# Last six rows as one-row chains, and no VectorE products in the last 16 rows, in a sum of reciprocals

## The chip, the core and the metric

One core of one Trainium2 chip. The metric is the device time of one execution in microseconds (us), smallest is best. Row numbers are those of one partition: each of the 128 partitions holds 128 rows of 1024 numbers, and "row 126" means row 126 of all partitions at once (0.5 MB).

## The reference

```python
def setup_inputs():
    batch, seq, dim = 32, 512, 1024
    return {"x": np.abs(np.random.randn(batch, seq, dim)).astype(np.float32) + 1e-6}

def reference(x):
    return np.sum(1.0 / x, axis=-1).astype(np.float32)
```

67.1 MB come in, 64 KB go out.

## The kernel before

A row's 1024 numbers are split into two halves of 512, a and b, and 1/a + 1/b is computed as (a + b) / (ab), so that ScalarE does its Ln and Exp on 512 products instead of 1024 numbers. Four engines share the rest:

- the product ab: GpSimd, or for some rows VectorE. For a product on VectorE, PE first puts b into PSUM (the memory that PE writes its results to) with two passes of an identity matrix (tile `b`);
- Ln and Exp(-.): ScalarE, giving 1/(ab), in PSUM (`r`) or in place (`pr`);
- the sum: either PE first adds a + b (four passes, tile `s`, in PSUM too) and VectorE multiplies and sums 512 numbers (0.68 us), or VectorE multiplies and sums all 1024 itself (1.22 us).

A chunk is a triple (m, e, v): m rows, of which e are added by PE, and v have their product on VectorE. Loads are lists of chunks; A, B and C are pairs of rows. All loads go into a ring of 40 rows.

```python
    SINGLE = 124
    A, B, C = (2, 0, 0), (2, 2, 0), (2, 2, 1)
    LOADS = [[A, B, A, B], [A, B, A, C]] * 5 + [[A, B, A, C]]
    LOADS += [[A, B], [A, C]] * 3 + [[A], [B], [A], [C]] * 2
    # (cut)
    for chunks in LOADS:
        n = sum(m for m, _, _ in chunks)
        xt = ring[:, c0 % R : c0 % R + n, :]
        keep(nc.sync.dma_start(out=xt, in_=x_v[:, c0 : c0 + n, :]))
        made, q = [], 0
        for m, e, v in chunks:
            pr = ppool.tile([P, m, H], f32, tag="ps" if e else "pr")
            for j in range(v):                      # products on VectorE
                b = bpool.tile([P, H], f32, tag="b")
                add(b, xt[:, q + j, H:])            # PE
                i = nc.vector.tensor_tensor(out=pr[:, j, :], in0=xt[:, q + j, :H], in1=b, op=mult)
            # (cut)
        for (m, e, v), pr in zip(chunks, made):
            # (cut) product of the other rows on GpSimd, then for e rows:
            #       add(s, xc[:, j, :H], xc[:, j, H:])   on PE
            if waiting:
                sum_rows(*waiting)                  # VectorE, chunk before
            keep(nc.scalar.activation(out=pr, in_=pr, func=Ln, scale=S))
            step = 1 if c0 + q >= SINGLE else m
            # (cut) Exp of the m - e other rows into PSUM, of the e rows in place
            waiting = c0 + q, xc, pr, sm, rc
```

Rows 0 to 111 come in loads of eight and four rows, rows 112 to 127 in eight loads of two. Each engine runs its own instructions in the order in which this loop makes them.

## Time and profile before

| | kernel before |
|---|---|
| time, median of 3 runs | 171.8 us (171.78 to 171.88) |
| span of the profiled run | 169.98 us |
| last load landed | 161.04 us |
| last sum on VectorE done | 167.10 us |
| output's store and closing after it | 2.88 us |

The first line of the page gives each engine's busy time and its share of the span:

```profile
PE 131.9 (78%) x278; PEld 50.8 (30%) x278; DVE 122.5 (72%) x267; ACT 134.1 (79%) x131; POOL 138.3 (81%) x70
```

No engine is full, because the loads are (93% of the span). In such a kernel a late change can only move what lies between the last landing and the end. I call that distance, from the last landing to the end of VectorE's last accumulator read, **the tail**: 6.06 us here.

### The profile page before, as it was taken

The page shows a single profiled execution, that of the slowest core. Times are in us where ns is not written, and L with a number is a line of the kernel's source. Part 1 is how long each engine was busy: PE and PEld are TensorE (multiplying, and loading weights), DVE is VectorE, ACT ScalarE, POOL GpSimd, SP SyncE. Part 2 cuts the span into 40 slices and gives each one's busy share as a digit, 9 for nine tenths or more (in the row PEclk, how much of TensorE's full clock was granted, in tenths as well). Part 3 has the DMA queues.
Part 4 walks back from the last instruction along what each step waited for, and adds up shares of the span by engine and source line. Part 5 has one row for each costly group of instructions (what it writes and reads, how often), then busy time and mean ns, then how long its engine had stood idle before and what let it go on. Part 6 is the DMA issues. An engine that isn't in the chain of part 4 may idle for free.

```text
span 170.0 us, 1264 instructions
## 1 busy us (share of the span) xinstructions
PE 131.9 (78%) x278; PEld 50.8 (30%) x278; DVE 122.5 (72%) x267; ACT 134.1 (79%) x131; POOL 138.3 (81%) x70
## 2 busy tenths in 40 slices
PE   0008899786988789784999869798879999998790
PEld 0003333231332233231443313233333334333230
DVE  0000777767987677767687679878789898989883
ACT  3002989978887988958889787888999999999890
POOL 1008999699996999689996998979999999998920
PEclk9999999999999999999599999999999999999999
DMA  6999999999999999999999999999999999999400
GB/s 208 409 455 409 463 401 463 409 455 409 463 411 455 409 455 405 447 418 440 424 440 424 440 424 441 397 420 422 428 432 432 428 416 418 414 422 428 175 0 15
DMA packets 3750, 67.24 MB, mean 396 GB/s; under 512 B 416, under 2 KB 544, under 8 KB 544
## 3 DMA queue, kind: packets, MB, share of 16 engines
q1 hardware_dynamic: 3744, 67.18, 92.9%
q8 instruction: 2, 0.03, 0.1%
q14 instruction: 4, 0.03, 0.0%
HBM read 67.11 MB, written 0.07 MB: 395 GB/s over the span
## 4 chain that ended last, share of the span: by engine, by line
DMA 63%; POOL 15%; ACT 10%; issue 4%; DVE 3%; PE 3%; DVEq 0%; POOLq 0%; SPq 0%
DMA ring<-in_x_dram 63%; POOL pr L143 15%; ACT pr L154 6%; PE s L84 2%; DVE ring L94 2%; ACT r L162 2%; ACT pr L169 2%; DVE pr L94 1%; PE b L84 1%; DVE pr L132 0%; DVEq L202 0%; DVE sums L94 0%; POOLq L143 0%; SPq L124 0%; DVEq L94 0%
## 5 line engine op out<-in xcount | busy, mean ns | idle before, releaser
L143 POOL TENSOR_TENSOR pr<-ring 128x1024 f32<-128x1024 f32 x64 | 137.6, 2185 | 23.5 <-DMA ring<-in_x_dram 23.2
L84 PE MATMUL s<-ring,ident 128*128 128x512 f32 x256 | 122.4, 616 | 32.2 <-DVE sums L94 16.2
L154 ACT ACTIVATE pr<-pr 128x1024 f32<-128x1024 f32 x64 | 67.3, 1052 | 28.6 <-POOL pr L143 28.5
L84 PEld LDWEIGHTS s<-ring,ident 128*128 128x128 f32 x256 | 46.8, 193 | 104.6 <-issue 62.1
L94 DVE CUSTOM_DVE_ANT_1 pr<-ring,r 128x1024 f32<-128x1024 f32 x31 | 37.9, 1221 | 43.3 <-ACT r L162 43.1
L94 DVE CUSTOM_DVE_ANT_0 pr<-pr,s 128x512 f32<-128x512 f32 x64 | 41.4, 684 | 0.6 <-PE s L84 0.5
L94 DVE CUSTOM_DVE_ANT_1 ring<-ring,r 128x1024 f32<-128x1024 f32 x33 | 40.1, 1217 | 0.0
L169 ACT ACTIVATE pr<-pr 128x1024 f32<-128x1024 f32 (+1 forms) x33 | 33.9, 1031 | 1.0
L162 ACT ACTIVATE r<-pr 128x1024 f32<-128x1024 f32 (+1 forms) x33 | 33.0, 1001 | 1.0
L84 PE MATMUL b<-ring,ident 128*128 128x512 f32 x22 | 12.3, 639 | 1.6 <-DMA ring<-in_x_dram 1.5
L94 DVE DVE_READ_ACCUMULATOR2_ANT sums<- 128x1 f32 x128 | 10.6, 83 | 0.0
L132 DVE TENSOR_TENSOR pr<-ring,b 128x512 f32<-128x512 f32 x11 | 7.5, 684 | 0.8 <-PE b L84 0.7
L84 PEld LDWEIGHTS b<-ring,ident 128*128 128x128 f32 x22 | 4.0, 201 | 9.4 <-DMA ring<-in_x_dram 7.5
L55 ACT ACT_TABLE_LOAD x1 | 1.3, 1283 | 0.7 <-PEq L191 0.7
masks.py:197 POOL MEMSET ident<- 128x128 f32 x1 | 0.2, 205 | 0.3 <-POOLq L191 0.3
masks.py:199 POOL TENSOR_SCALAR_AFFINE_SELECT ident<-ident 128x128 f32<-128x128 f32 x1 | 0.3, 294 | 0.1
L191 POOL MEMSET const-float32-0.0<- 128x1 f32 x1 | 0.1, 99 | 0.2 <-issue 0.2
L191 POOL MEMSET const-bfloat16-1.0<- 128x1 bf16 x1 | 0.1, 102 | 0.0
L191 POOL MEMSET const-uint8-127<- 128x1 uint8 x1 | 0.1, 102 | 0.0
L191 POOL MEMSET const-float32-1.0<- 128x1 f32 x1 | 0.1, 99 | 0.0
## 6 DMA issues: line engine op xcount, KB each, us to landing
ring<-in_x_dram SPq DMA_DIRECT2D x11, 4096.0 KB, 37.7
ring<-in_x_dram SPq DMA_DIRECT2D x6, 2048.0 KB, 36.8
ring<-in_x_dram SPq DMA_DIRECT2D x8, 1024.0 KB, 28.3
out_dram<-sums SPq DMA_DIRECT2D x1, 64.0 KB, 1.5
```

Source lines behind the costliest of these rows:

```text
L55: nc.scalar.add_instruction(mybir.InstLoadActFuncSet(name=nc.get_next_instruction_name(), act_func_set_id=act_sets.index("natural_log_exp_ ...
L84: i = nc.tensor.matmul(bank, lhsT=ident, rhs=half, start=k == 0, stop=k == len(halves) - 1,)
L94: i = nc.vector.tensor_tensor_reduce(out=row if out is None else out, in0=row, in1=fac, scale=S, scalar=0.0, op0=mult, op1=plus, accum_out ...
L132: i = nc.vector.tensor_tensor(out=pr[:, j, :], in0=xt[:, q + j, :H], in1=b, op=mult)
L143: i = nc.gpsimd.tensor_tensor(out=pr[:, v:, :], in0=xc[:, v:, :H], in1=xc[:, v:, H:], op=mult)
L154: keep(nc.scalar.activation(out=pr, in_=pr, func=Ln, scale=S))
L162: nc.scalar.activation(out=r, in_=pr[:, j:to, :], func=Exp, scale=-1.0)
L169: keep(nc.scalar.activation(out=r, in_=r, func=Exp, scale=-1.0))
L191: nc = _bacc.Bacc("TRN2", target_bir_lowering=False, num_devices=1)
```

## The change

The intent: the last rows pass through the engines one by one, so that the last row doesn't wait for its pair, and VectorE and PE are rid of the products in the last 16 rows (rows 118 and 126), which GpSimd takes instead.

```diff
-    SINGLE = 124
     A, B, C = (2, 0, 0), (2, 2, 0), (2, 2, 1)
+    L, S1 = (1, 0, 0), (1, 1, 0)
     LOADS = [[A, B, A, B], [A, B, A, C]] * 5 + [[A, B, A, C]]
-    LOADS += [[A, B], [A, C]] * 3 + [[A], [B], [A], [C]] * 2
+    LOADS += [[A, B], [A, C]] * 3 + [[A], [B], [A], [B], [A]]
+    LOADS += [[L, S1], [S1, S1], [L, S1]]
 (cut: the special case of SINGLE in sum_rows)
-            step = 1 if c0 + q >= SINGLE else m
             rc = []
-            for j in range(e, m, step):
 (cut: with one row to a chunk, one Exp of m - e rows and one of e rows do)
```

More of the change, by code (lines that the diff above doesn't have):

```diff
@@ L113, in sum_rows @@
                 rc[j - e].unsqueeze(1).to_broadcast([P, 2, H]),
-                pr[:, e : e + 2, :] if j == e and e + 1 < m and c < SINGLE else None,
+                pr[:, e : e + 2, :] if j == e and e + 1 < m else None,
             )
@@ L154 @@
             keep(nc.scalar.activation(out=pr, in_=pr, func=Ln, scale=S))
-            step = 1 if c0 + q >= SINGLE else m
             rc = []
-            for j in range(e, m, step):
-                to = min(j + step, m)
-                r = rpool.tile([P, to - j, H], f32, tag="rc")
+            if e < m:
+                r = rpool.tile([P, m - e, H], f32, tag="rc")
                 keep(
-                    nc.scalar.activation(
-                        out=r, in_=pr[:, j:to, :], func=Exp, scale=-1.0
-                    )
-                )
-                rc += [r[:, l, :] for l in range(to - j)]
-            for to in range(e, 0, -step):
-                r = pr[:, max(to - step, 0) : to, :]
+                    nc.scalar.activation(out=r, in_=pr[:, e:, :], func=Exp, scale=-1.0)
+                )
+                rc = [r[:, l, :] for l in range(m - e)]
+            if e:
+                r = pr[:, :e, :]
                 keep(nc.scalar.activation(out=r, in_=r, func=Exp, scale=-1.0))
```

## The prediction

> **What bounds the kernel now.** I read the page of the whole span first, then the chain that ended last, then the groups with shapes kept apart, then the last 30 us as a timeline by engine. The page, transfers by slice (40 slices of 4.25 us) and the load queue:
>
> ```profile
> DMA  6999999999999999999999999999999999999400
> q1 hardware_dynamic: 3744, 67.18, 92.9%
> ```
>
> The transfers never pause from the first slice until slice 37. The landing records of the last eight loads (two rows of each partition, 1 MB) stand at 143.67, 146.16, 148.65, 151.13, 153.62, 156.10, 158.58 and 161.04 us: one each 2.48 us, 1.24 us a row, 1.05 MB per 2.48 us = 423 GB/s. So the first 161.04 us are the memory's. The chain that ended last, in order of time, says what follows:
>
> ```profile
> 141.21 19.84 DMA ring<-in_x_dram
> 161.04 0.04 issue
> 161.09 1.12 PE b L84 x2
> 162.21 3.45 PE s L84 x8
> 165.66 0.03 issue
> ...
> 165.79 0.11 DVE pr L94
> ...
> 166.49 0.60 DVE pr L94
> 167.09 0.01 DVE sums L94
> ```
>
> The last load waits in the queue for 19.84 us, so nothing that compute does late in the kernel delays it. After it come PE's sum of one row's halves for VectorE's product (b), PE's sums of both last rows (s), then two sums on VectorE; the output leaves at 167.13, and 2.85 us of store and closing follow to 169.98. Only 167.10 - 161.04 = 6.06 us can be won here.
>
> Durations come from the groups by shape:
>
> ```profile
> L143 POOL TENSOR_TENSOR pr<-ring 128x1024 f32<-128x1024 f32 x53 | 124.2, 2372 | 23.4 <-DMA ring<-in_x_dram 23.2
> L94 DVE CUSTOM_DVE_ANT_0 pr<-pr,s 128x512 f32<-128x512 f32 x64 | 41.4, 684 | 0.6 <-PE s L84 0.5
> L169 ACT ACTIVATE pr<-pr 128x512 f32<-128x512 f32 x2 | 1.1, 622 | 0.0
> L162 ACT ACTIVATE r<-pr 128x512 f32<-128x512 f32 x2 | 1.1, 592 | 0.0
> L143 POOL TENSOR_TENSOR pr<-ring 128x512 f32<-128x512 f32 x11 | 14.1, 1283 | 0.1
> L132 DVE TENSOR_TENSOR pr<-ring,b 128x512 f32<-128x512 f32 x11 | 7.5, 684 | 0.8 <-PE b L84 0.7
> ```
>
> A product of two rows on GpSimd takes 2.37 us, of one row 1.28; in a row they start 2.33 and 1.24 apart (their records overlap by 0.04). The third view is GpSimd's timeline near the end:
>
> ```profile
> 141.26 11.86 POOL L143 TENSOR_TENSOR pr<-ring 128x1024 f32<-128x1024 f32 x6
> 153.75 8.72 POOL L143 TENSOR_TENSOR pr<-ring 128x1024 f32<-128x1024 f32 x4 [0.63 <-DMA ring<-in_x_dram]
> ```
>
> GpSimd ran behind the transfers until 153.12, then waited 0.63 us for rows 120 and 121. It catches up only because row 118's product was VectorE's: 2 rows cost it 1.24 us there, not 2.33. This slack is what the change spends.
>
> **What the Trainium skill says.** "ScalarE: Activation LUTs", section "What ACT_TABLE_LOAD costs", gives an activation with immediates as 186 ns + 0.833 ns per element, with about 93 ns of overlap back to back: 1039 ns for 1024 elements, 613 for 512. The trace agrees: 1028 to 1059 and 582 to 629. Halving the width thus doesn't halve the time. "GPSIMD Engine Reference", section "3.1 Elementwise — side-by-side cycle accounting", has about 2.6 cycles an element at two inputs, 2.17 ns at 1.2 GHz; the trace's (2372 - 1283) / 512 is 2.13 ns, which leaves 0.19 us for each instruction. "SBUF — State Buffer", section "SBUF: two separate sides", says that a VectorE instruction with two SBUF inputs shuts GpSimd out, and one with a PSUM input does not. Every two-input VectorE instruction here reads one input from PSUM, and all eleven short products of GpSimd took 1272 to 1295 ns, beside a busy VectorE: no blocking is seen. "DMA: Bandwidth & Descriptors", section "Measured (HBM→SBUF, 128 partitions, SWDGE, issued from GpSimd)", has 425 GB/s for a large transfer; 423 here from another issuing queue: the stream has no reserve.
>
> **The change part by part.** The order of instructions shows that rows 0 to 117 and the 25 loads (sizes and order) stay as they were; the two kernels differ from row 118 on.
>
> Removed: VectorE's products of rows 118 and 126 (2 x 0.68 us) and, on PE, their b sums (2 x 0.86 us: two passes per half at 0.43 us a start). The second one stands on the final chain. Of the last load, PE now sums row 127 alone: 4 passes, 1.72 us, instead of 12 passes. Rows summed on PE stay 64. So PE would be done near 163 if nothing else held it.
>
> Added to GpSimd: 2.33 - 1.24 = 1.09 us at rows 118/119; row 126's product, 1.24 us; and rows 122/123 and 124/125 as single products, (2 x 1.24 - 2.33) = 0.15 us each time. Together 2.63 us, of which its pauses after 153 (1.12 us by the single starts, 0.63 of them in the line above) take up a part. GpSimd, from the start of rows 118/119 at 151.85 in the trace: next starts 154.18 (rows 120/121), 156.51 (122), 157.75 (123), 158.99 (124), 160.23 (125), 161.47 (126), 162.71 (127), done 163.99 (162.48 + 2.63 - 1.12). Each of its rows has landed by then, so it never waits again; six single rows at 1.24 are exactly as fast as the transfers. In the kernel before its last product ended at 162.48.
>
> ScalarE: six more activations (131 to 137 instructions). A dependent pair starts Ln then Exp 0.66 us apart (0.63 and the 0.03 us hand-over seen from 163.27 + 1.04 to 164.34), and the next Ln 0.54 after that Exp (164.34 to 164.88 in the trace): 1.20 us a row against 2.05 for two rows. Rows 120/121: Ln at 156.58 after GpSimd, Exp 157.67. Row 122's Ln then waits for ScalarE, not GpSimd, and starts 157.67 + 0.97 = 158.64. From there 1.20 each: 123 at 159.84, 124 at 161.04, 125 at 162.24, 126 at 163.44, 127 at 164.64. Last Exp from 165.30 to 165.93.
>
> VectorE: rows 120/121 at 158.73 and 159.88, then row 122 at 161.02 (1.15 a start), 123 at 162.17, 124 at 162.78, 125 at 163.56 (its Exp), 126 at 164.73 (its Exp), 127 at 165.96, done with the read of the accumulator at about 166.65. That last start is set almost equally by ScalarE (165.96) and by VectorE's own row 126 (164.73 + 1.15 = 165.88). PE's sum of row 127 needs one of three buffers, the one row 123 frees at about 162.8: 162.85 + 1.72 + 0.17 = 164.7, before 165.9, so PE leaves the path.
>
> Sum: VectorE ends at 166.65 instead of 167.10, 0.45 us earlier. Off the path go about 4.6 us of PE; in their place stand GpSimd's lateness and ScalarE's six rows. 171.8 - 0.45 = 171.35.
>
> **The rivals.** First, that GpSimd is no queue at all and the tail is only landing, one product, Ln, Exp and sum: 161.04 + 2.52 + 1.3 + 0.7 = 165.5, a gain of 1.6 us (170.2). For it speaks the wait of 0.63 us at 153.12; against it that the change removes the cause of this wait. Second, that ScalarE's chain is slower than mine or that VectorE loses its overlap: the built order shows that the single-row sums on VectorE wait for PE, for ScalarE and for VectorE itself, one wait more than the two-row ones had. If each costs 0.1 us in VectorE's chain (the pause between wait and start at 165.69 to 165.79), or each Exp 0.1 us more, the gain is lost or turns into +0.3 us (172.1). Against it: these waits are for old work and are passed while ScalarE is waited for. Third, that PE's wait for row 123's buffer ends last; it has 1.2 us in hand, so VectorE would have to be that late. Fourth, that transfers stop earlier or later: the last load is issued at 141.21, before any changed row, so I give this nothing beyond 0.1 us of scatter (the three runs span 171.78 to 171.88).
>
> **Range and chances.** 171.4 us, half-way between my sum and the second rival's small costs. The range 170.7 to 172.0 takes in most of the first and second rival. For faster by over 2% the time must fall under 168.4, which needs 3.4 of the 6.06 us behind the last landing; two products of GpSimd, Ln, Exp and a sum alone are 4.5 us. Chance 0.01. Slower by over 2% needs 3.4 us more on some engine in the tail, 0.01. The rest, 0.98, is within 2%.
>
> **What would show each step.** Right: the last landing stays at 161.0 (within 0.1); GpSimd doesn't pause after 153 and ends at about 164.0; ScalarE runs without pause from about 158.6 to 165.9; VectorE's last sum ends at 166.4 to 166.9, and the final chain goes through ScalarE or GpSimd with no PE in it. Wrong: a landing that moved; a wait of GpSimd for a load after 154; PE's s among the last waits; single Ln or Exp far from 0.63 us; or a VectorE chain with gaps of over 0.1 us between sums whose Exp was ready.

## The result and the profile after

171.06 us (median of 6 runs, 170.92 to 171.21) against 171.84 (6 runs, 171.75 to 172.23): ratio 0.9951, 95% interval 0.9939 to 0.9964, within 2%. A ratio in this document is the mean time of one kernel's fast runs over that of the other's fast runs of the same rounds, so not quite the ratio of the medians. The gain is 0.8 us; the prediction's sum had been 0.45 us, its stated time 171.4.

The chain that ended last, from GpSimd's product of rows 120/121 on (start, duration, what):

```profile
154.12 2.40 POOL pr L144
156.52 0.02 issue
156.54 1.06 ACT pr L155
...
158.59 0.62 ACT pr L155
159.21 0.02 issue
159.24 0.60 ACT r L160
...
163.96 0.18 ACT r L160
...
164.69 0.20 DVE ring L95
...
165.92 0.60 DVE pr L95
166.52 0.01 DVE sums L95
```

PE is gone from it. GpSimd hands over to ScalarE at rows 120/121, and from 156.54 ScalarE does nothing but its own work to the end: Ln at 158.59 is row 122's, Exp at 163.96 row 126's. VectorE's two last sums follow. GpSimd's timeline shows that it no longer pauses for a load; one merged piece runs from 138.88 to 163.91:

```profile
138.88 25.03 POOL L144 TENSOR_TENSOR pr<-ring 128x1024 f32<-128x1024 f32 x14
```

PE's timeline for the last three rows that it adds; the second piece is row 127, which had to wait for a PSUM buffer (0.57 us by the bracket, until VectorE had read row 123's) and is still done at 164.85, before row 127's Exp:

```profile
158.62 3.67 PE L85 MATMUL s<-ring,ident 128*128 128x512 f32 x8 [0.53 <-DMA ring<-in_x_dram]
162.87 1.98 PE L85 MATMUL s<-ring,ident 128*128 128x512 f32 x4 [0.57 <-DVE sums L95]
```

The one-row instructions in the groups by shape (count, then busy us, mean ns, and idle us before them):

```profile
L144 POOL TENSOR_TENSOR pr<-ring 128x512 f32<-128x512 f32 x15 | 19.0, 1286 | 0.0
L155 ACT ACTIVATE pr<-pr 128x512 f32<-128x512 f32 x6 | 3.7, 613 | 0.0
L165 ACT ACTIVATE pr<-pr 128x512 f32<-128x512 f32 x4 | 2.5, 630 | 0.1
```

Every duration is the one that the prediction used, within 3%. The tail is 5.60 us (160.93 to 166.53), so the path from the last landing is worth 6.06 - 5.60 = 0.46 us, almost exactly the predicted 0.45. The remaining 0.3 to 0.4 us are not on that path. The span behind the last sum holds the store of the sums and a closing exchange between the engines; I call it **the closing**: 2.88 us before, 2.51 after. VectorE runs two drain instructions there: the first starts while its last sums run and ends 0.05 us behind them, the second is part of the exchange. In the listing of the closing's instructions, VectorE's drains read (least, middle, most ns of the two; first and last start in us):

```profile
L202 DVEq DRAIN  x2: 130/602/1074, 166.1 to 169.6; - x2
```

before, and after:

```profile
L198 DVEq DRAIN  x2: 19/392/764, 165.8 to 168.6; - x2
```

The last drain takes 19 ns instead of 130 and, counted from the last sum, starts 2.09 us instead of 2.53 us later. Nothing in the change is meant to do this. So the experiments had two questions: which part of the change is worth the 0.46 us, and where the closing's 0.37 us come from.

### The profile page after: what moved, and what is told of

It is laid out like the page before. It is cut to its first block, busy times and chain, and to the rows that moved or that the text cites. A ratio compares the mean times of both kernels' runs of the same rounds, so it can differ in the third digit from the quotient of the medians.

```text
span 169.0 us, 1265 instructions
## 1 busy us (share of the span) xinstructions
PE 130.5 (77%) x274; PEld 49.9 (30%) x274; DVE 121.1 (72%) x265; ACT 134.7 (80%) x135; POOL 140.7 (83%) x73
## 4 chain that ended last, share of the span: by engine, by line
DMA 52%; POOL 22%; ACT 13%; issue 8%; DVE 3%; POOLq 0%; DVEq 0%; SPq 0%
DMA ring<-in_x_dram 52%; POOL pr L144 22%; ACT pr L155 8%; ACT r L160 2%; ACT pr L165 2%; DVE ring L95 2%; DVE pr L95 1%; DVE pr L133 0%; DVE sums L95 0%; POOLq L144 0%; DVEq L198 0%; SPq L125 0%
## 5 line engine op out<-in xcount | busy, mean ns | idle before, releaser
L144 POOL TENSOR_TENSOR pr<-ring 128x1024 f32<-128x1024 f32 (+1 forms) x67 | 140.0, 2130 | 22.6 <-DMA ring<-in_x_dram 22.6
L155 ACT ACTIVATE pr<-pr 128x1024 f32<-128x1024 f32 (+1 forms) x67 | 67.9, 1013 | 28.2 <-POOL pr L144 28.2
L165 ACT ACTIVATE pr<-pr 128x1024 f32<-128x1024 f32 (+1 forms) x34 | 34.2, 1007 | 1.1
L85 PE MATMUL b<-ring,ident 128*128 128x512 f32 x18 | 10.0, 639 | 0.0
L133 DVE TENSOR_TENSOR pr<-ring,b 128x512 f32<-128x512 f32 x9 | 6.1, 683 | 0.7 <-PE b L85 0.7
L85 PEld LDWEIGHTS b<-ring,ident 128*128 128x128 f32 x18 | 3.4, 205 | 6.2 <-DMA ring<-in_x_dram 4.3
```

The costliest lines, as they stand in the source:

```text
L85: i = nc.tensor.matmul(bank, lhsT=ident, rhs=half, start=k == 0, stop=k == len(halves) - 1,)
L144: i = nc.gpsimd.tensor_tensor(out=pr[:, v:, :], in0=xc[:, v:, :H], in1=xc[:, v:, H:], op=mult)
L165: keep(nc.scalar.activation(out=r, in_=r, func=Exp, scale=-1.0))
```

## The experiments

Theory: the tail was PE's (two passes for b, eight for s, then two sums), the change replaces it by ScalarE's one-row chain, which starts late because GpSimd is late. Rivals: fewer VectorE products are worth something in themselves; PE's passes alone are the gain; GpSimd's last two products or the last landing still set the end; and for the rest of the time, scatter.

Twelve runs were made, eleven other kernels and the changed kernel again; all gave correct results, each timed in five rounds against nine runs of the kernel before on the same chip (three groups of four, on three chips). The edits of e1 and p1 are to the kernel before, that of p3 is to e2, all others are to the changed kernel; some are printed shortened. Tail and closing are from each kernel's one trace; records are the entries in VectorE's stream there, waits and drains included.

| run | median us (before) | ratio, 95% interval | tail us | VectorE records | closing us |
|---|---|---|---|---|---|
| kernel before | | | 6.06 | 321 | 2.88 |
| changed kernel | 171.06 (171.84) | 0.9951, 0.9939 to 0.9964 | 5.60 | 319 | 2.51 |
| e1, row 118 to GpSimd only | 171.71 (171.75) | 0.9992, 0.9979 to 1.0004 | 6.06 | 319 | 2.57 |
| e2, row 118 back on VectorE | 170.83 (171.75) | 0.9944, 0.9931 to 0.9956 | 5.23 | 321 | 2.81 |
| e3, single rows in the last load only | 171.87 (171.75) | 1.0006, 0.9993 to 1.0018 | 6.36 | 319 | 2.50 |
| e4, row 126 back on VectorE | 172.00 (171.75) | 1.0007, 0.9993 to 1.0020 | 6.28 | 321 | 2.81 |
| changed kernel again | 171.08 (171.83) | 0.9958, 0.9944 to 0.9971 | 5.55 | 319 | 2.51 |
| e5, pairs exchanged | 170.88 (171.83) | 0.9943, 0.9930 to 0.9955 | 5.38 | 319 | 2.50 |
| e6, e2 with loads of one row | 170.91 (171.83) | 0.9946, 0.9933 to 0.9958 | 5.21 | 321 | 2.87 |
| e7, rebalanced | 171.23 (171.83) | 0.9964, 0.9952 to 0.9977 | 5.87 | 323 | 2.51 |
| p1, before + 2 memsets | 171.46 (171.85) | 0.9978, 0.9965 to 0.9990 | 6.06 | 323 | 2.57 |
| p2, changed + 2 memsets | 171.28 (171.85) | 0.9968, 0.9955 to 0.9980 | 5.59 | 321 | 2.81 |
| p3, e2 + 2 memsets | 170.71 (171.85) | 0.9931, 0.9919 to 0.9944 | 5.25 | 323 | 2.51 |
| p4, spread | 170.72 (171.85) | 0.9932, 0.9918 to 0.9945 | 5.13 | 324 | 2.52 |

In each of these runs, the change of the tail plus the change of the closing gives the measured difference of mean times to within 0.2 us (least well in e3, -0.08 against +0.11 us, and e1, -0.31 against -0.13). So one trace's tail and closing say where the time goes, but not to the hundredth.

### e1: row 118's product to GpSimd, nothing else

```diff
-    LOADS += [[A, B], [A, C]] * 3 + [[A], [B], [A], [C]] * 2
+    LOADS += [[A, B], [A, C]] * 3 + [[A], [B], [A], [B], [A], [B], [A], [C]]
```

> The kernel before with one part of the change: row 118's product goes to GpSimd; the last eight rows stay two-row chains with row 126's product on VectorE. My theory (the end is PE's b and s passes after the last landing): GpSimd starts rows 120/121 at about 154.2 instead of 153.75 and no longer pauses, but its last product still ends by about 162.5 and PE's path (161.05 + 12 passes) is untouched, so the last sum ends 6.0 to 6.1 us after the last landing as in the kernel before: 171.8 us, ratio 0.998 to 1.001. Rival (fewer VectorE products and PE passes are worth something by themselves): VectorE ends 0.2 us or more earlier, ratio 0.997 or less.

Tail 6.06 us, as before to the hundredth; ratio 0.9992, whose interval holds 1 (the closing is 0.31 us shorter in the trace, of which the time shows 0.13). GpSimd's timeline has lost its pause:

```profile
141.39 21.27 POOL L143 TENSOR_TENSOR pr<-ring 128x1024 f32<-128x1024 f32 x10
```

So this half of the change buys nothing on the path while PE sets the end: the freed 0.68 us of VectorE and two passes of PE at row 118 lay off that path. The rival falls.

### e2: the change with row 118 left on VectorE

```diff
-    LOADS += [[A, B], [A, C]] * 3 + [[A], [B], [A], [B], [A]]
+    LOADS += [[A, B], [A, C]] * 3 + [[A], [B], [A], [C], [A]]
```

> The changed kernel with row 118's product given back to VectorE; only the last six rows are changed. My theory: GpSimd's lateness of 0.5 us goes, ScalarE starts rows 120/121 at about 156.24 instead of 156.54 (it is held by row 118's late product on VectorE, so not all of the 0.5 is won) and all its later single rows move by the same 0.30 us: last sum 0.3 us earlier than in the changed kernel, 5.3 us after the last landing, about 170.75 us, ratio 0.993 to 0.995. Rival (the move of row 118 is part of the gain): later than the changed kernel, 171.2 or more.

Tail 5.23 us, 0.37 less than in the changed kernel; 170.83 us. ScalarE's first and last one-row activations, with every one of them in between moved alike:

```profile
158.25 0.61 ACT L155 ACTIVATE pr<-pr 128x512 f32<-128x512 f32 x1
...
164.80 0.63 ACT L165 ACTIVATE pr<-pr 128x512 f32<-128x512 f32 x1
```

In the changed kernel these stand at 158.59 and 165.14, 0.34 later, and the tail follows. The move of row 118 to GpSimd is thus the harmful half of the change: it makes GpSimd 0.4 us late for rows 120/121 (154.12 instead of 153.68), ScalarE's one-row chain starts 0.34 us later, and since the chain then runs without a pause at 1.18 us a row in both kernels, it stays late to the end. In the time most of this is hidden: e2's closing is 0.30 us longer than the changed kernel's (see p1 to p3), and the intervals of the two ratios overlap.

### e3: single rows in the last load only

The code of the changed kernel, with rows 112 to 125 in the pairs of the kernel before:

```diff
-    LOADS += [[A, B], [A, C]] * 3 + [[A], [B], [A], [B], [A]]
-    LOADS += [[L, S1], [S1, S1], [L, S1]]
+    LOADS += [[A, B], [A, C]] * 3 + [[A], [B], [A], [C], [A], [B], [A]]
+    LOADS += [[L, S1]]
```

> The kernel before with single-row chains in the last load alone (row 126's product on GpSimd, row 127 summed through PE); rows 112 to 125 as before. It takes PE's b sums and one row of s off the final path, as the change does. Rival that PE's path alone is the gain: the same 0.6 us earlier end as the changed kernel, ratio 0.995. My theory: rows 124/125 are then two 1.15 us sums on VectorE that start when their pair's Exp ends at about 163.25, row 126 (1.15) follows at 165.55 and row 127 at 166.7: VectorE ends at 167.4, 0.3 us later than before, ratio 1.001 to 1.003. So the single rows 122 to 125 with their 0.6 us sums would be needed.

Tail 6.36 us, 0.3 longer than before. VectorE's timeline shows the reason:

```profile
163.24 1.22 DVE L95 CUSTOM_DVE_ANT_1 pr<-ring,r 128x1024 f32<-128x1024 f32 x1 [1.13 <-ACT r L160]
...
164.39 1.22 DVE L95 CUSTOM_DVE_ANT_1 ring<-ring,r 128x1024 f32<-128x1024 f32 x1
...
165.53 1.22 DVE L95 CUSTOM_DVE_ANT_1 ring<-ring,r 128x1024 f32<-128x1024 f32 x1
...
166.67 0.68 DVE L95 CUSTOM_DVE_ANT_0 pr<-pr,s 128x512 f32<-128x512 f32 x1
```

Rows 124, 125 and 126 are three long sums in a row, and they start only when the pair 124/125 leaves ScalarE at 163.2 (the bracket says that VectorE sat 1.13 us waiting for it). Taking PE off the end alone makes VectorE the bound, so the rival that PE's passes alone are the gain falls. The time itself (ratio 1.0006) hides a part of this loss, because this kernel's closing is 0.38 us shorter than that of the kernel before; see p1.

### e4: the change with row 126's product back on VectorE

```diff
-    LOADS += [[L, S1], [S1, S1], [L, S1]]
+    D1 = (1, 0, 1)
+    LOADS += [[L, S1], [S1, S1], [D1, S1]]
```

> The changed kernel with row 126's product put back on VectorE through two PE passes (b), nothing else. PE reaches these passes after row 125's s, so b ends at about 163.1, the product at 163.8, and row 126's Ln starts there instead of 163.3; GpSimd's last product ends 1.2 us earlier and is of no use. My theory: last sum 0.4 to 0.5 us later than in the changed kernel, VectorE ends at about 167.0, ratio 0.998. Rival (GpSimd's last two products set the end): 0.5 us or more earlier than the changed kernel, ratio 0.992 or less.

Tail 6.28 us, 0.68 more than the changed kernel: the direction held, the size was 0.2 short. VectorE's product and the Ln of row 126 that waits for it:

```profile
163.46 0.68 DVE L134 TENSOR_TENSOR pr<-ring,b 128x512 f32<-128x512 f32 x1
```

```profile
164.18 0.63 ACT L156 ACTIVATE pr<-pr 128x512 f32<-128x512 f32 x1 [0.64 <-DVE pr L134]
```

PE's passes for it ended at 163.32, and VectorE, in order behind its sums of rows 123 and 124, took the product at 163.46; ScalarE stood still for 0.64 us. The rival that GpSimd's last two products set the end falls: here GpSimd was done a row earlier, at 162.80, and the end came later. Of the change's parts, this one, row 126's product off PE and VectorE, is needed.

### The changed kernel again

> The changed kernel unaltered, to settle what its end is worth. The traces account for 0.46 us on the path from the last landing to the last sum (6.06 to 5.60), while the timed runs differ by 0.84 us. My theory: the rest is scatter of the start and of the closing (2.88 us in the one trace, 2.51 in the other, and 2.5 to 2.9 in the four experiments with no relation to the kernel), so on this chip the ratio lies nearer to 0.997 and the last sum is again 5.5 to 5.7 us after the last landing. Rival (the change also shortens the stream or the closing): ratio 0.995 again, with a closing near 2.5.

Ratio 0.9958, between my theory's 0.997 and the rival's 0.995, with the interval 0.9944 to 0.9971 holding both; tail 5.55 and closing 2.51, exactly that of the first trace. The closing was therefore no scatter, and this half of my theory fell. Laying the traces side by side then showed the column of VectorE records in the table: the four traces with 321 records close in 2.81 to 2.88 us, the six others of that time in 2.50 to 2.57. p1 to p3 test this.

### e5: no single rows before 126, the kinds of pair exchanged

```diff
-    LOADS += [[A, B], [A, C]] * 3 + [[A], [B], [A], [B], [A]]
-    LOADS += [[L, S1], [S1, S1], [L, S1]]
+    LOADS += [[A, B], [A, C]] * 3 + [[A], [B], [A], [C], [B], [A], [B]]
+    LOADS += [[L, S1]]
```

> As the run with single rows in the last load alone, which ended 6.35 us after the last landing, but with the two kinds of pair exchanged in rows 120 to 125: PE sums rows 120, 121, 124 and 125, and VectorE takes its two 1.15 us sums at rows 122 and 123. No single rows before row 126. If the late end of that run came from VectorE's long sums of rows 124/125 and not from the lack of single rows, VectorE starts row 126 at about 164.5 and row 127 at about 165.7, set by ScalarE: last sum 5.3 us after the last landing, 170.8 us, ratio 0.994 to 0.995, as good as the best single-row version. Rival (single rows from 122 on are what helps): 6.0 us or more, ratio 0.999 or above.

Tail 5.38 us, a full 0.98 less than e3, though rows 120 to 125 are pairs in both. So one-row chains for rows 122 to 125 are not what most of the gain needs (e2, which has them, has a tail only 0.15 us shorter); what helps is that the rows next to the last load have their short sums (through PE) and not two long ones on VectorE. The one-row chains of the change did that in passing, since its rows 123 to 125 are S1.

### e6: e2 with the last load cut in two

```diff
-    LOADS += [[L, S1], [S1, S1], [L, S1]]
+    LOADS += [[L, S1], [S1, S1], [L], [S1]]    # with [A], [C], [A] ahead, as in e2
```

> The run with row 118 on VectorE, with its last load split into two loads of one row, so that row 126 lands 1.2 us earlier and row 127 no later. Theory that ScalarE's chain of 1.18 us a row sets the end: rows 126 and 127 start their Ln when ScalarE is free (163.0 and 164.2), as without the split; last sum 5.1 to 5.3 us after the last landing, ratio within 0.001 of that run. Rival that the landing of the last load, or GpSimd's two products after it, still sets the end: 1 us or more earlier, ratio 0.989 or less.

Row 126 landed at 159.75 instead of 160.96, row 127 at 160.99, and ScalarE's Ln of the two rows stayed where it was:

```profile
162.98 0.61 ACT L155 ACTIVATE pr<-pr 128x512 f32<-128x512 f32 x1
...
164.16 0.61 ACT L155 ACTIVATE pr<-pr 128x512 f32<-128x512 f32 x1
```

e2 has both lines at the same hundredths. Tail 5.21 against 5.23, ratio 0.9946 against 0.9944. So the last landing does not set the end. GpSimd did not move either (its last product ends at 163.66 in e2 and 163.67 here), so this run doesn't test it. But that end lies 0.5 us before ScalarE starts the row's Ln at 164.16. With the one-row chain, ScalarE's queue of six rows sets the end.

### e7: a version meant to beat both, and its miss

```diff
-    LOADS += [[A, B], [A, C]] * 3 + [[A], [B], [A], [B], [A]]
-    LOADS += [[L, S1], [S1, S1], [L, S1]]
+    Q = (2, 1, 1)
+    LOADS += [[A, B], [A, C]] * 3 + [[B], [A], [Q], [B], [A], [C]]
+    LOADS += [[L, L], [S1, S1]]
```

> A version meant to beat both. Rows 112 to 123 stay pairs, with a VectorE product at rows 116 and 122 instead of 118, so that GpSimd has caught up with the loads at 118; rows 124 and 125 single without PE sums, rows 126 and 127 single with PE sums of 0.6 us on VectorE. Worked out step by step with the durations of the traces: ScalarE takes rows 124 to 127 from 160.2 on at 1.18 us a row, last Exp at 165.0, VectorE's last sum 4.7 us after the last landing: 170.4 us, ratio 0.991 to 0.993. Rival (something not in this working, such as the three PE buffers, row 127's PE sum landing at 164.8 or VectorE's two long sums at 124 and 125, ends last): 5.2 us or more, no better than the run with row 118 on VectorE.

Tail 5.87, not 4.7. My working had taken PE and VectorE as free at row 112; by the trace PE began that row's sum at 147.06, 3.4 us after it had landed (143.67), and VectorE was at the sums of rows 108 to 111 until 149.4. VectorE's product of row 122 and the Ln behind it:

```profile
158.52 0.68 DVE L133 TENSOR_TENSOR pr<-ring,b 128x512 f32<-128x512 f32 x1
```

```profile
159.30 1.06 ACT L155 ACTIVATE pr<-pr 128x1024 f32<-128x1024 f32 x1
```

So ScalarE's one-row chain began at 161.35 where I had 160.2, and those 1.15 us are the miss.

### p1, p2, p3: two memsets on VectorE

The same insertion in the kernel before (p1), the changed kernel (p2) and e2 (p3); VectorE waits for the first loads at that time:

```diff
     make_identity(nc, ident)
+    spare = opool.tile([P, 2], f32)
+    for k in range(2):
+        nc.vector.memset(spare[:, k : k + 1], float(k))
```

> The kernel before with two tiny memsets on VectorE at the start, where it is idle; nothing else. In the ten traces so far the closing from the last sum to the end is 2.81 to 2.88 us in the four whose VectorE stream has 321 records, and 2.50 to 2.57 in the six with 319 or 323; in the four, VectorE's last drain starts 0.36 us later and takes 127 to 130 ns instead of 19. Theory that the length of VectorE's stream decides this: with 323 records the kernel before closes in 2.5 us and is 0.35 us faster, 171.4 us, ratio 0.9975 to 0.9985, with the last sum still 6.06 us after the last landing. Rival (scatter, or something else of the kernel before): ratio 1.000, closing 2.88.

> The changed kernel with the same two memsets: 321 records. Theory of the stream's length: the closing grows from 2.51 to 2.85 us, last sum still 5.55 to 5.6 us after the last landing, 171.4 us, ratio 0.9970 to 0.9980, which is what the path alone is worth. Rival: unchanged, ratio 0.9955, closing 2.5.

> The run with row 118 on VectorE (321 records, closing 2.81) with the two memsets: 323 records. Theory of the stream's length: closing 2.5, last sum 5.2 us after the last landing, 170.5 us, ratio 0.992 to 0.993, the fastest so far. Rival: 170.85, ratio 0.9945.

All three closings went as the stream's length says, in both directions: 2.88 to 2.57 (321 to 323 records), 2.51 to 2.81 (319 to 321) and 2.81 to 2.51 (321 to 323), with the tails where they were (6.06, 5.59, 5.25). VectorE's drains of p1 and then of p2 in the closing:

```profile
L205 DVEq DRAIN  x2: 19/368/717, 166.4 to 169.2; - x2
```

```profile
L201 DVEq DRAIN  x2: 120/442/764, 165.9 to 169.1; - x2
```

In time: p1 is 0.4 us faster than the kernel before by doing more (ratio 0.9978, its interval without 1), and every one of its five spans (169.6 to 169.8) lies under every one of the nine beside it (169.9 to 170.3). p2 loses part of the change's gain; its interval overlaps that of the changed kernel, but its spans (169.4 to 169.7) start where those of the changed kernel's eleven runs, on other chips, end (169.0 to 169.4). p3 reached 170.71, not the expected 170.5, with a ratio of 0.9931 as against 0.992 to 0.993 expected.

What is shown is that the number of instructions in VectorE's stream moves the closing by 0.3 us (0.31, 0.30 and 0.29). The other 0.06 us of the change's 0.37 are SyncE's: between the landing of the store and its first drain it passes three waits in the kernel before, e1, e6 and p1 and two in all other traces, and that drain starts 1.82 us behind the last sum instead of 1.75 to 1.76.

Why the stream's length counts is open. In all five traces with 321 records the last drain is the 320th record of the stream, in the others the 318th, 322nd or 323rd; something that comes in blocks of instructions would fit, but only four lengths were seen, and no run looked into it. The traces hold a hint. The DMA's instruction queue moves single packets of 8 KB. With nothing but the two memsets added (p1), the packet at 117.61 us comes at 115.86, and the last one, which starts 0.33 us after the end in the kernel before, starts at 167.10, as the last sum ends. In all five traces with 321 records the last packet starts 0.31 to 0.33 us after the end, in the five with 319 records 1.08 to 1.09 us after it, and in the four with 323 or 324 records 2.6 to 3.1 us before it, when VectorE has reached record 319 or 320. So this packet goes with VectorE's stream, and its turn falls on the last drain just where the closing is long. It starts 0.65 to 0.68 us after the late drain, though, so it is not what the drain waited for.

### p4: a second version meant to beat all

```diff
-    LOADS += [[A, B], [A, C]] * 3 + [[A], [B], [A], [B], [A]]
-    LOADS += [[L, S1], [S1, S1], [L, S1]]
+    W = (2, 1, 0)
+    LOADS += [[A, B], [A, C]] * 3 + [[W], [A], [C], [W], [A], [C]]
+    LOADS += [[L, L], [S1, S1]]
```

> A second attempt at a version that beats all, after the rebalanced one missed because VectorE's product of row 122 came late (159.2) and held ScalarE. Rows 112 and 118: one row of the pair summed through PE and one on VectorE; pairs at 116 and 122 with one product on VectorE; 124 and 125 single without PE, 126 and 127 single with PE. Worked out step by step with the lateness of VectorE and PE at row 112 as the traces have it: row 122's product at 158.1, ScalarE takes rows 124 to 127 from 160.2 on, last sum 4.7 to 5.0 us after the last landing; with 324 records a closing of 2.5: 170.2 to 170.5 us, ratio 0.990 to 0.9925. Rival (VectorE is again late at the products and holds ScalarE): 5.5 us or more, ratio 0.995 or above.

Tail 5.13, the shortest of all, but not the 4.7 to 5.0 expected; 170.72 us and ratio 0.9932, the same as p3 and not the 0.990 to 0.9925 expected. Two of its timeline's lines, the first row of ScalarE's chain and VectorE's last sum:

```profile
160.88 0.61 ACT L155 ACTIVATE pr<-pr 128x512 f32<-128x512 f32 x1
```

```profile
165.73 0.69 DVE L95 CUSTOM_DVE_ANT_0 pr<-pr,s 128x512 f32<-128x512 f32 x1 [0.32 <-ACT pr L165]
```

Against the 161.29 of its last landing, ScalarE's chain begins 0.41 us before it, where I had 0.8 us (160.2 before 161.0); the end is again ScalarE's. Row 122's product on VectorE came at 158.05, as expected (158.1). But that product (0.68 us), the hand-over to ScalarE and the pair's Ln and Exp (2.06 us from start to the next start) lead from there to 160.88, so the expected 160.2 did not follow from its own step. p3 and p4 beat the kernel before by 0.7% and the changed kernel by about 0.2 to 0.3% (their ratios, 0.9931 and 0.9932, against 0.9951 and 0.9958 in other groups; not timed side by side).

## Why the prediction was right, point by point

| step of the prediction | predicted | trace of the changed kernel |
|---|---|---|
| last landing unchanged | 161.04 | 160.93 |
| GpSimd starts rows 120/121 | 154.18 | 154.12 |
| GpSimd ends its last product | 163.99 | 163.90 |
| ScalarE starts row 122 | 158.64 | 158.59 |
| ScalarE per single row | 1.20 | 1.18 |
| PE done with row 127 | 164.7 | 164.85 |
| VectorE starts rows 126, 127 | 164.73, 165.96 | 164.69, 165.84 |
| last accumulator read ends | 166.65 | 166.53 |
| from the store's issue to the end (taken as unchanged) | 2.85 | 2.48 |

**The path.** The mechanism and its size held: 0.45 us predicted, 0.46 (first trace), 0.51 (repeat) and 0.47 (p2) measured. Agreement to a hundredth is partly luck: ScalarE's rows took 1.18 us instead of 1.20, and an extra wait at row 126 (below) gave about as much back. That ScalarE's chain would set the end was confirmed by e6 (an earlier landing changed nothing) and e2 (an earlier chain moved the end by as much). One count was wrong: "six more activations (131 to 137 instructions)" are four (131 to 135), since the kernel before already took the Exps of rows 124 to 127 singly; no step used the count. That row 126's product on PE and VectorE was the cost of the old tail was confirmed by e4 (putting it back costs 0.68 us), though taking it off alone wins nothing (e3). That GpSimd's slack "is what the change spends" was confirmed by e2, at 0.37 us.

**The term that was mis-sized.** The sum of the prediction ended in "VectorE ends at 166.65 instead of 167.10, 0.45 us earlier", and then subtracted this from 171.8; it carried the 2.85 us of "store and closing" over unchanged. They measured 2.48 us. The change happens to shorten VectorE's stream from 321 records to 319, and p1 and p2 show that this length alone moves the closing by 0.3 us; the rest is SyncE's one wait less. 0.46 + 0.37 makes 0.83 us; the medians differ by 0.78, the ratio gives 0.84.

**The rivals.** The first (no queue on GpSimd, 170.2 us) failed as argued: GpSimd never paused. The second (an extra 0.1 us in each sum of VectorE) appeared once, at row 126. Its Exp, and VectorE's sum of it:

```profile
163.96 0.60 ACT L160 ACTIVATE r<-pr 128x512 f32<-128x512 f32 x1
```

```profile
164.69 1.22 DVE L95 CUSTOM_DVE_ANT_1 ring<-ring,r 128x1024 f32<-128x1024 f32 x1 [0.56 <-issue]
```

The Exp ended at 164.56 and the sum started 0.13 us later, behind one more wait instruction of VectorE's; row 125's sum had started 0.03 us after its Exp (163.41, 163.44). A gap of over 0.1 us was one of the prediction's signs of being wrong. It cost 0.04 us at most, since row 127's Exp ended only at 165.77 and its sum started at 165.84. The sums of rows 122 to 124 had no such gap: they started 1.15 and 0.60 us apart. The second rival's weight had pulled the stated 171.4 up from the 171.35 of the sum; the result lay on the other side. The third (PE's wait for row 123's buffer) happened, with 0.57 us on PE, and cost nothing, as predicted. Of the fourth (transfers that stop earlier or later), the last landing shows 0.11 us.

**What the prediction did not see.** It took the two halves of the change as one. e1, e2 and e5 show that they pull in opposite directions: moving row 118 costs 0.37 us once ScalarE sets the end, and single rows before row 126 are worth little (0.15 us between e5 and e2) if the last pairs are ordered well.

## What to carry to other kernels

When the stream of loads is full, only the tail behind the last landing counts; write it out engine by engine with start-to-start times, and look first for the engine that still works off a queue when the last data lands. Giving the last rows the cheapest work on each in-order engine helped more here than making the pieces smaller, and moving work to an engine that had only just caught up with the loads cost 0.37 of the 0.83 us that the tail could have won (6.06 to 5.23). Before a difference of a few tenths of a microsecond is explained by the work, check the closing: two memsets, run while VectorE was idle, moved it by 0.3 us, against the 0.46 us that the change won on the path.

## What the Trainium skill lacked or had wrong

- "VectorE: DVE Perf Modes", section "The DRAIN you can't avoid", has the drains of preamble and postamble as constant, at about 12 ns. VectorE's last drain took 19 ns in nine traces and 120 to 130 ns in five, and in those five the closing was 2.81 to 2.88 us instead of 2.50 to 2.57.
- That the closing depends on the number of VectorE's instructions (319, 323 and 324 records short, 321 long, 0.3 us apart with the rest alike) stands on no page that I found. That instruction packets follow VectorE's stream is seen under p1 to p3; whether the fetch of instructions is behind the late drain, no run here shows.
- "ScalarE: Activation LUTs", section "What ACT_TABLE_LOAD costs", gives the overlap of activations back to back (93 ns; here 0.07 to 0.10 us), but not the hand-over of a dependent pair: 0.03 us after the end of the first, so Ln to Exp 0.65 us and Exp to the next Ln 0.53 us at 512 elements.
